# Modulation products moved between TensorE and VectorE in a two-layer attention, S5 and MLP kernel

## The chip, the cores and the metric

The kernel runs on one core of a Trainium2 chip. The metric is the device time of one execution in microseconds (us). TensorE does the matrix products, VectorE and ScalarE the element-wise work, SyncE issues nearly all loads, and 16 DMA engines move the data. In the profile PE is TensorE's matmul row, PEld its weight loads, DVE is VectorE, ACT ScalarE, POOL GpSimd, SP SyncE.

## What is computed

256 tokens of width 2048 go through two blocks. The first has two layers (differential attention, then forgetting attention), the second an S5 mixer with a GLU and a squared-ReLU MLP of width 8192. Each stage is modulated by vectors that come from products of one row with a wide matrix:

```python
mod = c_act @ w_mod[l] + b_mod[l]              # 2048 x 6144, for layer 0 and layer 1
shift, scale, gate = jnp.split(mod, 3, axis=-1)
h = x * (1.0 + scale[:, None]) + shift[:, None]
...
mod = c_act @ w_mod_kv + b_mod_kv              # keys' and values' stage, 2048 x 4096
...
sh1, sc1, gt1, sh2, sc2, gt2 = adaln(c, w_mod[layer], b_mod[layer])          # 2048 x 12288
csh1, csc1, cgt1, csh2, csc2, cgt2 = adaln(c_ctx, w_mod[layer], b_mod[layer])
```

The change is about where these products are made, and when.

## The kernel before, in words

**Weights.** All other matrices are streamed in tiles of 128 columns, called weights here: 64 for layer 0's input, 16 for its output, 16 for the keys and 16 for the values, 32 for layer 1's heads (two a head), 16 for its output, 32 for the GLU, 128 for the MLP. Each comes as two loads `w` of 512 KB; ScalarE makes a rounded copy `wh` (L134), VectorE the rest `wl` (L135), and TensorE multiplies (L163 to L165, `mm_t`; L200 to L202, `mm_n`; L176 and L177 in the MLP). Weights are prepared two ahead of their use.

**Modulation products.** Each product of 2048 outputs is cut in two halves of 1024 outputs, and each half in eight pieces. A piece is two loads `graw` of 128x1024 (L268, 512 KB each) and what is done with them (`gemv`):

- "pe": eight matmuls into `g` (L222), four at a time beside each other in column groups of 32. The profile has 16 records for one piece, since a float32 matmul has two.
- "dve": two operations `gacc <- graw, csilu, gacc` of 1024 columns on VectorE (L237); the first one of a half is on ScalarE (L235). A half that has any such piece closes with four matmuls of `gacc` (L246).
- The context's products (`mc`, with two result rows) are on TensorE whatever is asked for: `if eng == "pe" or nv == 2`.

There are 224 pieces in one queue, in the order m0 (32 pieces, layer 0's scale and shift), m02 (16), mk (32, keys), m1 (32), mc (32, context), m12 (16), m22 (16), m24 (32), m25 (16).

**When.** `weights()` calls `bg()` once for each weight. `bg` takes the next entry of the stage's policy (`P_L0A` for the first four heads of layer 0, `POL0` for its last four, `P_ON0` for its output, `P_KV` for keys and values, `P_QG` for layer 1's heads, `P_ON1` for its output, `P_GLU`, `P_MLP`): an engine's name issues the next piece, `None` issues none. The loads go out at once, the use of a piece one piece later. Some more pieces are issued at fixed places: 32 at the start, 6 before the keys (`BG_K`), 12 at the S5 scan (`BG_M`), `BG_V` after each of the first `BG_B` blocks of the S5 outputs. There are four buffers for `graw`.

**Context states.** When the last mc piece is used, `start_ctx` (asked at the start of each of layer 1's 16 heads) starts `ctx_states`: 41 steps, one for each later weight, with matmuls `inc` (L697) and VectorE operations on `ctx_ws` (L1337 to L1340); what is left is done after layer 1's output (`flush`).

**Between stages** VectorE makes the next stage's input tile by tile: `xres` (L1112, L1113) and `kL` (L420) before the keys; `U` (L1599), `xres` (L1600), `xn` (L1612) and `h` (L420) before the MLP.

The order in which one engine's instructions stand is set when the program is built, by a scheduler that lays all of them out; each engine then runs its own queue in order.

## Time and profile before

| | us |
|---|---|
| runs, unprofiled: median of three | 2543.52 (2540.8 to 2544.13) |
| the profiled execution: its own time | 2548.22 |
| its span in the trace | 2546.4 |
| TensorE busy | 2377.1 (93%) |
| VectorE busy | 1776.8 (70%) |
| ScalarE busy | 1239.5 (49%) |

The span is what the trace covers; 1.8 us of the profiled execution lie around it. Busy shares are means over stages with different limits, so each stage is read by its own window.

### The profile page before, as it was taken

The page shows a single profiled execution, that of the slowest core. Times are in us where ns is not written, and L with a number is a line of the kernel's source. Part 1 is how long each engine was busy: PE and PEld are TensorE (multiplying, and loading weights), DVE is VectorE, ACT ScalarE, POOL GpSimd, SP SyncE. Part 2 cuts the span into 40 slices and gives each one's busy share as a digit, 9 for nine tenths or more (in the row PEclk, how much of TensorE's full clock was granted, in tenths as well). Part 3 has the DMA queues.
Part 4 walks back from the last instruction along what each step waited for, and adds up shares of the span by engine and source line. Part 5 has one row for each costly group of instructions (what it writes and reads, how often), then busy time and mean ns, then how long its engine had stood idle before and what let it go on. Part 6 is the DMA issues. An engine that isn't in the chain of part 4 may idle for free.

```text
span 2546.4 us, 47968 instructions
## 1 busy us (share of the span) xinstructions
PE 2377.1 (93%) x18854; PEld 2051.9 (81%) x18854; DVE 1776.8 (70%) x3360; ACT 1239.5 (49%) x2153; POOL 118.8 (5%) x234
## 2 busy tenths in 40 slices
PE   5699999999899999999998874999899999999997
PEld 1299999999678888988886663898688888888885
DVE  3288778877775555778788997877854565665655
ACT  0554554444365556666653543544544443443442
POOL 0000000000002110000000021000000000000000
PEclk9999999999889999999998886999899999999998
DMA  9999999878769998878786762998366666666652
GB/s 325 339 344 325 323 321 344 306 275 316 265 226 342 327 332 290 296 248 290 257 273 230 233 210 77 334 320 279 118 186 187 186 187 191 189 190 184 189 182 91
DMA packets 203316, 644.66 MB, mean 253 GB/s; under 512 B 41009, under 2 KB 49457, under 8 KB 202705
## 3 DMA queue, kind: packets, MB, share of 16 engines
q1 hardware_dynamic: 195616, 620.47, 72.7%
q0 software_dynamic: 7472, 21.11, 2.1%
q8 instruction: 148, 2.42, 0.4%
q14 instruction: 80, 0.65, 0.1%
HBM read 613.71 MB, written 25.69 MB: 251 GB/s over the span
## 4 chain that ended last, share of the span: by engine, by line
PE 84%; DVE 9%; DMA 3%; ACT 2%; issue 1%; SPq 0%; POOL 0%; DVEq 0%; ACTq 0%; POOLq 0%
PE pj L176 18%; PE pj L163 12%; PE pj L164 12%; PE pj L165 12%; PE pj L177 9%; PE g L222 3%; PE pjv L200 3%; DMA graw<-in_w_mod 3%; PE pjv L201 2%; PE pjv L202 2%; DVE scan_t L1415 2%; DVE scan_t L1417 2%; DVE S L1419 2%; PE inc L697 2%; PE st L370 1%
## 5 line engine op out<-in xcount | busy, mean ns | idle before, releaser
L135 DVE TENSOR_TENSOR wl<-w,wh 128x1024 fp32r<-128x1024 f32 x631 | 770.0, 1224 | 465.2 <-ACT wh L134 457.2
L134 ACT CAST wh<-w 128x1024 fp32r<-128x1024 f32 x632 | 659.1, 1050 | 711.1 <-PE pj L176 283.0
L176 PE MATMUL pj<-h,wh 128*128 128x512 f32 x1024 | 362.9, 399 | 6.8 <-DVE h L420 5.0
L176 PE MATMUL pj<-d,wh 128*128 128x512 f32 x1024 | 360.3, 398 | 0.0
L237 DVE SCALAR_TENSOR_TENSOR gacc<-graw,csilu,gacc 128x1024 f32<-128x1024 f32 x211 | 270.2, 1281 | 27.4 <-DMA graw<-in_w_mod 18.6
L177 PE MATMUL pj<-h,wl 128*128 128x256 f32 x1024 | 287.5, 281 | 1.1 <-DVE wl L135 1.1
L177 PE MATMUL pj<-d,wl 128*128 128x256 f32 x1024 | 285.8, 280 | 0.0
L176 PEld LDWEIGHTS pj<-h,wh 128*128 128x128 f32 x1024 | 193.1, 189 | 55.8 <-issue 4.0
L176 PEld LDWEIGHTS pj<-d,wh 128*128 128x128 f32 x1024 | 192.0, 188 | 48.2 <-PE pj L177 1.7
L163 PE MATMUL pj<-hH,wh 128*128 128x256 f32 x768 | 221.6, 289 | 6.2 <-ACT hH L419 4.0
L165 PE MATMUL pj<-hH,wl 128*128 128x256 f32 x768 | 221.4, 289 | 0.5 <-DVE wl L135 0.5
L164 PE MATMUL pj<-hL,wh 128*128 128x256 f32 x768 | 221.1, 288 | 0.0
L222 PE MATMUL g<-graw,czc 128*32 128x256 f32 x1744 | 168.4, 469 | 49.6 <-DMA graw<-in_w_mod 48.0
L177 PEld LDWEIGHTS pj<-h,wl 128*128 128x128 f32 x1024 | 194.0, 189 | 1.5 <-DVE wl L135 1.5
L177 PEld LDWEIGHTS pj<-d,wl 128*128 128x128 f32 x1024 | 193.1, 189 | 0.4
L163 PEld LDWEIGHTS pj<-hH,wh 128*128 128x128 f32 x768 | 148.8, 194 | 9.8 <-ACT hH L419 4.1
L165 PEld LDWEIGHTS pj<-hH,wl 128*128 128x128 f32 x768 | 148.6, 194 | 4.5 <-issue 3.3
L164 PEld LDWEIGHTS pj<-hL,wh 128*128 128x128 f32 x768 | 148.9, 194 | 3.8 <-issue 3.7
L222 PEld LDWEIGHTS g<-graw,czc 128*32 128x32 f32 x1744 | 46.0, 119 | 129.4 <-DMA graw<-in_w_mod 105.5
L163 PE MATMUL pj<-h1H,wh 128*128 128x256 f32 x512 | 147.1, 290 | 0.3 <-ACT ctx_ws L1323 0.2
L164 PE MATMUL pj<-h1L,wh 128*128 128x256 f32 x512 | 146.4, 287 | 0.0
L165 PE MATMUL pj<-h1H,wl 128*128 128x256 f32 x512 | 146.0, 286 | 0.0
(480 smaller groups left out, 5201.4 us busy)
## 6 DMA issues: line engine op xcount, KB each, us to landing
graw<-in_w_mod SPq DMA_DIRECT2D x384, 512.0 KB, 5.8
w<-in_mlp_in SPq DMA_DIRECT2D x128, 512.0 KB, 4.3
w<-in_mlp_out SPq DMA_DIRECT2D x128, 512.0 KB, 4.3
w<-in_a_in SPq DMA_DIRECT2D x96, 512.0 KB, 6.3
graw<-in_w_kvmod SPq DMA_DIRECT2D x64, 512.0 KB, 6.6
w<-in_b_in SPq DMA_DIRECT2D x64, 512.0 KB, 5.8
w<-in_glu SPq DMA_DIRECT2D x56, 512.0 KB, 5.3
w<-in_a_v SPq DMA_DIRECT2D x32, 512.0 KB, 5.9
```

The lines of the kernel that those rows point to most:

```text
L134: nc.scalar.copy(h, src)
L135: (eng or (nc.gpsimd if next(self.spl) else nc.vector)).tensor_sub(l, src, h)
L163: self.nc.tensor.matmul(ps, h, aH, start=kt == order[0] and not opened, stop=False)
L164: self.nc.tensor.matmul(ps, h, aL, start=False, stop=False)
L165: self.nc.tensor.matmul(ps, l, aH, start=False, stop=kt == order[-1] and last)
L176: self.nc.tensor.matmul(ps, h, view(aH, 0, [[T, 2], [1, T]]), start=kt == order[0], stop=False)
L177: self.nc.tensor.matmul(ps[:, 0], l, aH, start=False, stop=kt == order[-1])
L200: self.nc.tensor.matmul(ps[:, i], aH[:, s], h, start=half == 0 and i == 0 and k == 0, stop=False)
L201: self.nc.tensor.matmul(ps[:, i], aH[:, s], l, start=False, stop=False)
L202: self.nc.tensor.matmul(ps[:, i], aL[:, s], h, start=False, stop=half == 1 and i == 1 and k == 7)
L222: nc.tensor.matmul(st["g"][32 * q:32 * q + 32], self.cz[c][:, ch * 2 + s], raw[s][:, q * 256:q * 256 + 256], start=st["n"] == 0, stop=ch = ...
L237: nc.vector.scalar_tensor_tensor(acc, raw[s], cc, acc, op0=MUL, op1=ADD)
```

## The change

Five policies and two numbers change, an entry of a policy may now be a tuple (several pieces at one weight), and layer 1's heads get a second policy, `P_QG2`, once the context's products are done.

```diff
-P_L0A = ('dve', 'pe')
-P_KV = ('dve', 'pe')
-P_QG = ('dve', 'dve', 'pe')
+P_L0A = ('dve', 'dve', 'dve', None)
+P_KV = ('dve',)
+P_QG = (('pe', 'pe'), 'pe')
+P_QG2 = ('dve', 'dve', None)
...
-P_ON1 = ('pe', 'dve', None)
-BG_V = 5
+P_ON1 = ('dve', None, None)
+BG_V = 2
...
-BG_B = 0
+BG_B = 3
...
             e = eng or next(self.pol)
-            if e and self.bgq and not (self.hold and self.bgq[0][0].startswith("m2")):
+            for e in e if isinstance(e, tuple) else (e,):
+                if not e or not self.bgq or self.hold and self.bgq[0][0].startswith("m2"):
+                    continue
                 name, gen, left = self.bgq[0]
...
                 self.steps = itertools.cycle(P_CTX)
+                self.policy(P_QG2, X_QG)
```

`P_L0A`, `P_KV`, `P_GLU` and the other policies are asked once for each weight, so the pieces can be counted:

| stage (weights) | before: pieces, of these on TensorE | changed: pieces, of these on TensorE |
|---|---|---|
| start | 32, 32 | 32, 32 |
| layer 0, heads 0 to 3 (32) | 32, 16 | 24, 0 |
| layer 0, heads 4 to 7 (32) | 24, 0 | 24, 0 |
| its output (16), then 6 | 18, 0 | 18, 0 |
| keys and values (32) | 32, 29 | 32, 18 |
| layer 1's heads (32) | 32, 14 | 30, 15 |
| its output (16) | 11, 6 | 6, 0 |
| S5 | 3 on VectorE and 12, 12 | 2 on VectorE and 18, 18 |
| GLU (32) | 28, 0 | 32, 0 |
| MLP (128) | 0, 0 | 6, 0 |

VectorE's queue between layer 0's output and the keys: `xres` and `kL` make the keys' input, `vprod` and `gen_ws` belong to a table of the S5 part, `lnb` is the layer norm's row. Before, at the eighth and ninth of the 16 tiles:

```order
L1113 TENSOR_TENSOR xres<-xres,lnb 128x256
L1112 TENSOR_TENSOR xres<-xres,lnb 128x256
L420 TENSOR_TENSOR kL<-u,kH 128x256
L635 TENSOR_TENSOR gen_ws<-vprod 128x32x16
L1113 TENSOR_TENSOR xres<-xres,lnb 128x256
L1112 TENSOR_TENSOR xres<-xres,lnb 128x256
L420 TENSOR_TENSOR kL<-u,kH 128x256
L554 TENSOR_TENSOR vprod<-gen_ws 128x512
```

In the changed program at the eighth tile (a line has a number there that is up to four higher):

```order
L557 TENSOR_TENSOR vprod<-gen_ws 128x512
L558 TENSOR_TENSOR vprod<-gen_ws 128x512
L238 SCALAR_TENSOR_TENSOR gacc<-graw,csilu,gacc 128x1024
L1116 TENSOR_TENSOR xres<-xres,lnb 128x256
L1115 TENSOR_TENSOR xres<-xres,lnb 128x256
L423 TENSOR_TENSOR kL<-u,kH 128x256
L638 TENSOR_TENSOR gen_ws<-vprod 128x32x16
L238 SCALAR_TENSOR_TENSOR gacc<-graw,csilu,gacc 128x1024
```

Between the norm's mean (`mr`) and the last `kL` there stood 8 operations `gacc`; now there are 16, one for nearly every tile.

VectorE's queue between the GLU and the MLP: `rr` is the end of a chain of small operations on 2 columns, and `U`, `xres`, `xn`, `h` make the MLP's input from it. Before:

```order
L1594 COPY rr<-ry 128x2
L1599 SCALAR_TENSOR_TENSOR U<-U,gs_18449,rrb 128x256
L1600 TENSOR_TENSOR xres<-xres,U 128x256
L1612 TENSOR_TENSOR xn<-xres,rrb 128x256
L1599 SCALAR_TENSOR_TENSOR U<-U,gs_18449,rrb 128x256
L1600 TENSOR_TENSOR xres<-xres,U 128x256
L1612 TENSOR_TENSOR xn<-xres,rrb 128x256
```

Changed:

```order
L1598 COPY rr<-ry 128x2
L238 SCALAR_TENSOR_TENSOR gacc<-graw,csilu,gacc 128x1024
L1603 SCALAR_TENSOR_TENSOR U<-U,gs_18214,rrb 128x256
L238 SCALAR_TENSOR_TENSOR gacc<-graw,csilu,gacc 128x1024
L1604 TENSOR_TENSOR xres<-xres,U 128x256
L238 SCALAR_TENSOR_TENSOR gacc<-graw,csilu,gacc 128x1024
L1616 TENSOR_TENSOR xn<-xres,rrb 128x256
L1603 SCALAR_TENSOR_TENSOR U<-U,gs_18214,rrb 128x256
L238 SCALAR_TENSOR_TENSOR gacc<-graw,csilu,gacc 128x1024
```

From the GLU's last `xy` to the fourth `U` no `gacc` stood there before; 15 stand there now: the pieces that are left over from the GLU, and the six that the MLP's policy issues.

SyncE's queue, the loads of the MLP's first weights (`w_0` and `w_1` are the two halves of one weight), changed program:

```order
L131 DMA w_1_20682<-in_mlp_in 128x1024
L269 DMA graw<-in_w_mod 128x1024
L131 DMA w_0_20729<-in_mlp_in 128x1024
L269 DMA graw<-in_w_mod 128x1024 x12
L131 DMA w_1_20735<-in_mlp_in 128x1024
```

Twelve loads `graw` now stand ahead of the second half of the MLP's fifth weight; before, the last `graw` stood ahead of the MLP's first weight.

## Rows read from the trace of the kernel before

**Rows 1.** Page: busy time by engine; the chain that ended last, by engine.
```profile
PE 2377.1 (93%) x18854; PEld 2051.9 (81%) x18854; DVE 1776.8 (70%) x3360; ACT 1239.5 (49%) x2153; POOL 118.8 (5%) x234
...
PE 84%; DVE 9%; DMA 3%; ACT 2%; issue 1%; SPq 0%; POOL 0%; DVEq 0%; ACTq 0%; POOLq 0%
```

**Rows 2.** Windows by stage: PE, PEld, DVE, ACT, POOL busy; clock, DMA share, GB/s.
```profile
301.70:362.20 60.50, 60.50 (x528) 55.97 (x528) 49.09 (x81) 31.02 (x56) 4.71 (x10) 1.00 0.94 333
...
698.00:720.00 22.00, 17.11 (x72) 15.03 (x73) 22.00 (x44) 10.55 (x23) 0.56 (x1) 0.58 0.69 212
...
749.00:780.00 31.00, 31.00 (x329) 27.46 (x322) 22.90 (x35) 21.80 (x43) 7.23 (x16) 1.00 0.98 348
...
841.00:964.00 123.00, 123.00 (x1293) 107.30 (x1289) 70.40 (x97) 64.53 (x123) 20.22 (x45) 1.00 0.96 332
964.00:1029.00 65.00, 65.00 (x553) 55.45 (x551) 34.81 (x59) 40.44 (x83) 6.46 (x12) 1.00 0.86 298
...
1490.00:1566.00 76.00, 45.02 (x416) 38.26 (x416) 76.00 (x373) 18.96 (x36) 18.00 (x24) 0.77 0.33 100
...
1777.00:1810.00 33.00, 20.68 (x90) 15.25 (x89) 26.00 (x76) 15.96 (x29) 0.00 (x0) 0.74 0.22 68
```

**Rows 3.** Windows of L222 alone, TensorE's modulation products: PE, PEld busy.
```profile
180.00:241.00 61.00, 5.11 (x64) 1.26 (x64) 1.00 0.92 319
...
749.30:841.10 91.80, 12.95 (x180) 5.05 (x176) 1.00 0.97 337
...
1241.80:1375.00 133.20, 7.12 (x96) 2.96 (x96) 1.00 0.78 262
```

**Rows 4.** Windows of VectorE alone, four weights of layer 0 each.
```profile
150.10:180.00 29.90, 27.13 (x42) 1.00 1.01 362
...
211.90:241.00 29.10, 25.71 (x42) 1.00 0.89 305
...
332.70:362.20 29.50, 25.70 (x44) 1.00 0.91 330
```

**Rows 5.** Timeline of VectorE before the keys: start us, us; idle before, releaser.
```profile
714.02 1.29 DVE L237 SCALAR_TENSOR_TENSOR gacc<-graw,csilu,gacc 128x1024 f32<-128x1024 f32 x1
715.22 0.43 DVE L1113 TENSOR_TENSOR xres<-xres,lnb 128x256 f32<-128x256 f32 x1
...
732.18 0.76 DVE L420 TENSOR_TENSOR kL<-u,kH 128x256 fp32r<-128x256 f32 x2 [0.17 <-ACT kH L419]
```

**Rows 6.** Timeline of TensorE there: the last wait on VectorE.
```profile
724.91 0.53 PE L165 MATMUL pj<-kH,wl 128*128 128x256 f32 x1 [1.19 <-DVE wl L135]
```

**Rows 7.** Timeline of VectorE at layer 1's end: the context's last operations, two norm steps.
```profile
1362.68 0.69 DVE L1337 TENSOR_TENSOR ctx_ws<-ctx_ws 128x512 f32<-128x512 f32 x1
1363.29 0.69 DVE L1338 TENSOR_TENSOR ctx_ws<-ctx_ws 128x512 f32<-128x512 f32 x1
...
1369.55 0.42 DVE L1337 TENSOR_TENSOR ctx_ws<-ctx_ws 128x256 f32<-128x256 f32 x1
1369.88 0.42 DVE L1338 TENSOR_TENSOR ctx_ws<-ctx_ws 128x256 f32<-128x256 f32 x1
...
1380.44 0.16 DVE L332 SCALAR_TENSOR_TENSOR rq<-rq,lv 128x2 f32<-128x2 f32 x1
1380.64 0.16 DVE L333 SCALAR_TENSOR_TENSOR rq<-rq 128x2 f32<-128x2 f32 x1
```

**Rows 8.** Chain that ended last, layer 1's heads: start us, us.
```profile
1044.64 1.90 PE inc L697 x32
```

**Rows 9.** Timeline of VectorE between GLU and MLP: start us, us; idle before, releaser.
```profile
1783.44 0.16 DVE L385 TENSOR_SCALAR var<-ysum 128x2 f32<-128x2 f32 x1 [2.95 <-PE ysum L380]
...
1789.32 0.48 DVE L1599 SCALAR_TENSOR_TENSOR U<-U,gs,rrb 128x256 f32<-128x256 f32 x1 [1.31 <-PE rrb L343]
...
1819.30 0.42 DVE L420 TENSOR_TENSOR h<-u,h 128x256 fp32r<-128x256 f32 x1 [0.77 <-ACT h L419]
```

**Rows 10.** All of `graw`: from issue to landing.
```profile
DMA to landing us min/median/max: 3.5/5.9/12.3
```

## The prediction

> **What bounds the kernel now.** I read the page first, then windows stage by stage, then the timelines of the places where stages meet. The page says TensorE: busy 93% of the span, and 84% of the chain that ended last, against 9% for VectorE [rows 1]. The windows split this. In the heads of layer 0, in the keys' and values' stage and in layer 1's heads TensorE is busy all the time (60.50 of 60.50 us, 31.00 of 31.00, 123.00 of 123.00, 65.00 of 65.00), at full clock [rows 2]. There a record taken from TensorE shortens the stage, as long as VectorE and the loads keep up; the reader should note that neither has much room: VectorE is at 81% in a head of layer 0, and the DMA share is 0.93 to 0.98. In three other stretches VectorE sets the pace: before the keys (698 to 720 us: VectorE 22.00 of 22.00, TensorE at a granted 0.58), in the scan (1490 to 1566: 76.00 of 76.00), and between GLU and MLP (1777 to 1810: 26.00 of 33.00, TensorE at 0.74) [rows 2]. What is put into VectorE's queue there is paid in full, unless it falls into a wait.
>
> **What the change moves.** By the count of the policies TensorE loses 16 pieces in layer 0, 11 in the keys' and values' stage and 6 in layer 1's output; it gains 1 in layer 1's heads and 6 in S5. The title's words don't hold in full: the start's 32 pieces stay on TensorE, and so do the 18 pieces of the context that come up among keys and values. VectorE gets what TensorE loses, and eight pieces of layer 0 pass down the line, until ten more come up in the GLU and the MLP.
>
> **Prices.** A piece on TensorE is 16 records: 5.11/64 x 16 = 1.28 us in layer 0, where it is split in two, 12.95/180 x 16 = 1.15 among keys and values, 7.12/96 x 16 = 1.19 in layer 1's output [rows 3]. An operation `gacc` takes VectorE 1.20 us from its start to the next one's (714.02 to 715.22), and a piece is two [rows 5].
>
> **The sum, term by term** (minus is faster).
>
> a) Layer 0, heads 0 to 3: 16 x 1.28 = -20.5. VectorE takes 24 pieces in place of 16, some 16 operations more. They come three pieces at a run and then none, so I look at four weights at a time. In the changed order 7, 8 and 7 operations stand in three such stretches that had 3 each; VectorE was busy 27.13 of 29.90, 25.71 of 29.10 and 25.70 of 29.50 us in them [rows 4]. With 4, 5 and 4 times 1.20 more it needs 31.9, 31.7 and 30.5 us, while TensorE, without two pieces, needs 27.3, 26.5 and 26.9: 13.4 us too much, if nothing is handed on to the neighbours, which have room. I take about half, 6: **-14.5**, bounds -20.5 and -7.1.
>
> b) Before the keys: 8 more operations in the row that makes `kL`, 9.6 us. TensorE waits for this row up to 724.91 [rows 6], the last `kL` starts at 732.18 [rows 5], so the last of them press less: **+8.4**, bounds 4.8 (the half that stands early) and 9.6.
>
> c) Keys and values: 11 x 1.15 = -12.7. The DMA share is 0.98 in the keys' part and 0.96 in the values' part [rows 2]; the same loads in less time leave hardly anything, and I give 2.7 back: **-10**, bounds -12.7 and -2.
>
> d) Layer 1's heads: one piece more, 1.2. Nine weights now carry 14 pieces. The stretch had a DMA share of 0.86 at 298 GB/s [rows 2], so the bytes fit, but four buffers must serve pairs, and a load takes 5.9 us to land [rows 10]. Half a landing in all, 3: **+4.2**, bounds 1.2 and 9.
>
> e) Layer 1's output: 6 x 1.19: **-7.1**, bounds -7.1 and -4. VectorE has no more pieces there than before.
>
> f) The context starts one head later, as its last piece is used at the tenth weight in place of the seventh. Two weights fewer are left for its steps, so its last block runs into the norm after layer 1's output: 4 or 5 operations of 0.61 us, 4 of 0.33, and as many each at about half of this and less [rows 7], some 6.5 us. Against it stand one `gacc` (1.20) that was there, and gaps of the norm's small operations, which start 0.20 apart and last 0.16 [rows 7], about 1.5 over some 28 of them. 16 matmuls `inc`, 1.90 us [rows 8], move from a stretch where TensorE is full to one where it waits. 6.5 - 1.2 - 1.5 - 1.9 = 1.9: **+1.9**, bounds 0 and 5.
>
> g) S5: the 6 added pieces stand in TensorE's queue behind the first blocks' outputs, while VectorE still scans; TensorE is busy 45.02 of 76.00 us there [rows 2]. **0**; without that cover 6 x 1.15 = 6.9.
>
> h) Between GLU and MLP: 15 operations `gacc` now stand in the one chain that the MLP waits for. Two waits can hide one or two, 2.95 us for `ysum` and 1.31 for `rrb` [rows 9]; 13 x 1.20 = 15.6 remain. Their loads come through four buffers, four in 5.9 + 1.2 us, which is 1.8 each and slower than 1.20 only where no other operation stands between. **+16**, bounds 12 (three more hidden) and 24 (every one waits for its load). TensorE can't take it back: the MLP's input is complete when the last `h` starts at 1819.30 [rows 9], and from there it is TensorE's own stage. The twelve loads ahead of the MLP's fifth weight cost nothing: four weights and a half are in before them, and TensorE needs several us for each.
>
> Sum: -14.5 + 8.4 - 10 + 4.2 - 7.1 + 1.9 + 0 + 16 = -1.1. Against the profiled execution's 2548.2 us that is 2547.1; that execution lay 4.7 above the median of the runs, 2543.5, so on their scale the changed kernel comes to **2542 us**: what TensorE is relieved of is handed back where VectorE sets the pace.
>
> **The rule that speaks otherwise.** The rows show VectorE full and TensorE at half its pace in exactly the places that get the most operations [rows 2]. The Trainium skill, Perfetto Trace Analysis, section "Identifying the Most-Contended Engine", says that a kernel is improved by improving the engine with the highest occupancy, which is TensorE here. By that alone the sum would be a, c, d and e without their deductions, -20.5 - 12.7 + 1.2 - 7.1 = -39, or 2504 us.
>
> **Rivals.** A measurement of this kernel tells a difference of about 0.2%, 5 us, from none.
>
> *No change, as summed:* 0.36.
>
> *The queues absorb it:* the deductions in a, c and d don't appear, since weights are prepared two ahead and VectorE can lag by that much. For it speaks that TensorE never waits in layer 0 with VectorE at 91% (27.13 of 29.90 [rows 4]). Sum: -20.5 + 8.4 - 12.7 + 1.2 - 7.1 + 1.9 + 16 = -12.8, 2531 us: 0.30.
>
> *VectorE becomes the bound of layer 0's first four heads* (the other side): VectorE's queue holds the splits `wl` and each head's softmax, which TensorE needs, behind `gacc`. If the overrun grows to eat the whole -20.5, a is 0 and the sum +13.4, 2557 us; from a = -8.4 on the kernel is more than 5 us slower. Against it: over a whole head the load is (49.09 + 4 x 1.20)/(60.50 - 5.11) = 97%, which is high but still under 1 [rows 2, 3]. 0.20.
>
> *Pairs of pieces wait for their loads* in layer 1's first nine weights: 14 pieces at 1 us of TensorE's time each, in place of the 3 in all, make it 2553 us. Against it: the DMA share of 0.86. 0.10.
>
> *Everything comes back that TensorE is relieved of* (that rule as a mechanism: b, f and h find waits to hide in): 2504 us. The waits that rows 9 show are 4.3 us, not 26. 0.04.
>
> **The range.** The two middle cases and the larger part of the next two lie within 2528 to 2557; what is left out is the last case and the outer parts of the second, third and fourth, under 2 in 10. For the likeliest case alone I would write 2538 to 2548. Faster by over 0.2%: 0.30 + 0.04 = 0.34; within it: 0.36; slower: 0.20 + 0.10 = 0.30.
>
> **What would show it.** a: heads 1 to 3 at some 56 to 58 us each in place of 60.5, with TensorE's first waits for `wl`. b: the weights of the keys start as before, and the fifth begins some 8 us later, measured from the first. c: the values' part little changed, the keys' part shorter by 4 to 10 us. f: `ctx_ws` between `mr` and the last `ry` of layer 1's norm. g: scan and S5 outputs as long as before. h: 33 us from the last GLU matmul to the full MLP grow to about 49; this is the step that I hold surest. The prediction is wrong if heads 0 to 3 lose less than 7 us, or if the stretch before the MLP grows by less than 10.

## The result, and the profile after

The changed kernel takes 2576.4 us (median; 2574.37 to 2578.54) against 2542.8 us: a ratio of 1.0133, 95% interval 1.0121 to 1.0146, so 33.6 us slower. The forecast was 2542 us, no change, with a range of 2528 to 2557. The profiled execution took 2575.43 us with a span of 2573.7, 27.3 us longer than the span before. The other 6.4 us lie between profile and median: the profiled execution of before was 5.4 us above its runs, this one 1.0 below.

TensorE was relieved, as the change says, and VectorE loaded. The page's first row, to compare with [rows 1]:

```profile
PE 2358.2 (92%) x18430; PEld 2045.4 (79%) x18430; DVE 1830.9 (71%) x3413; ACT 1240.4 (48%) x2152; POOL 124.4 (5%) x234
```

TensorE is busy 18.9 us less and the kernel is slower all the same. The Trainium skill, Perfetto Trace Analysis, section "Identifying the Most-Contended Engine", would have the engine with the highest occupancy optimized first. By the whole span that is TensorE, and here 18.9 us less of its busy time went with 27.3 us more of span. The Trainium skill, Perfetto Trace Analysis, section "Optimization Strategy", says that a kernel can have several regimes whose most contended engine changes, and with that the trace agrees, as the stages show.

Windows by stage, each from the first matmul of one stage to that of the next; layer 1's heads are also shown in two parts, which meet at their thirteenth weight. First the changed kernel (us; then PE, PEld, DVE, ACT, POOL busy; clock, DMA share, GB/s):

```profile
115.70:342.30 226.60, 220.45 (x1803) 215.40 (x1804) 199.82 (x282) 124.42 (x212) 17.89 (x32) 0.97 0.92 331
342.30:379.80 37.50, 31.96 (x256) 31.11 (x255) 33.95 (x61) 20.55 (x42) 5.33 (x8) 0.91 0.73 267
...
688.20:735.50 47.30, 37.23 (x197) 33.29 (x197) 44.29 (x78) 22.13 (x44) 1.99 (x5) 0.68 0.75 247
735.50:819.90 84.40, 84.30 (x831) 79.30 (x832) 71.27 (x94) 59.19 (x112) 16.76 (x31) 1.00 0.84 296
819.90:948.80 128.90, 124.53 (x1266) 105.83 (x1264) 68.90 (x92) 64.07 (x119) 20.12 (x41) 0.99 0.92 330
948.80:1249.80 301.00, 288.37 (x2480) 251.29 (x2480) 209.97 (x375) 181.88 (x376) 10.74 (x28) 0.96 0.77 258
948.80:1076.30 127.50, 122.27 (x1102) 98.46 (x1102) 63.41 (x112) 71.43 (x153) 9.49 (x26) 0.94 0.84 290
1076.30:1249.80 173.50, 166.11 (x1381) 152.83 (x1379) 146.57 (x264) 110.45 (x224) 1.25 (x2) 0.98 0.72 234
1249.80:1384.00 134.20, 130.32 (x1112) 113.21 (x1111) 100.99 (x176) 71.65 (x134) 3.70 (x6) 0.99 0.73 243
1384.00:1605.90 221.90, 149.63 (x1905) 114.68 (x1905) 195.08 (x883) 98.41 (x190) 31.26 (x40) 0.78 0.54 181
...
1766.00:1854.00 88.00, 61.99 (x367) 50.69 (x365) 77.83 (x138) 38.79 (x66) 0.53 (x2) 0.79 0.64 224
```

The same stages of the kernel before, where [rows 2] show only a part of them:

```profile
112.20:362.20 250.00, 245.06 (x2085) 225.55 (x2086) 197.75 (x307) 128.54 (x231) 17.93 (x38) 0.99 0.94 335
362.20:390.60 28.40, 28.40 (x250) 27.14 (x250) 16.78 (x21) 14.08 (x23) 1.43 (x4) 1.00 0.93 331
...
698.10:749.30 51.20, 44.46 (x309) 38.38 (x309) 40.70 (x79) 28.89 (x59) 2.00 (x5) 0.77 0.59 182
749.30:841.10 91.80, 91.80 (x966) 80.69 (x962) 58.80 (x84) 55.92 (x108) 18.50 (x40) 1.00 0.97 337
841.10:964.00 122.90, 122.90 (x1293) 107.30 (x1289) 70.40 (x97) 64.44 (x123) 20.12 (x45) 1.00 0.96 331
964.00:1241.80 277.80, 277.10 (x2403) 244.77 (x2401) 205.41 (x360) 183.13 (x377) 8.80 (x18) 0.99 0.83 280
964.00:1066.10 102.10, 101.93 (x905) 88.10 (x903) 61.52 (x98) 70.70 (x148) 6.46 (x12) 1.00 0.84 290
1066.10:1241.80 175.70, 175.17 (x1500) 156.67 (x1499) 143.89 (x263) 112.43 (x229) 2.34 (x6) 0.99 0.82 274
1241.80:1378.10 136.30, 134.24 (x1192) 115.12 (x1190) 106.19 (x198) 67.66 (x123) 2.44 (x6) 1.00 0.78 265
1378.10:1592.20 214.10, 143.35 (x1805) 113.44 (x1805) 192.29 (x861) 98.21 (x188) 31.38 (x38) 0.76 0.53 171
...
1752.70:1823.20 70.50, 56.34 (x354) 47.77 (x352) 54.76 (x118) 36.99 (x63) 0.00 (x0) 0.88 0.41 132
```

| stage | before | changed | difference | predicted |
|---|---|---|---|---|
| layer 0, first 36 weights (a) | 278.4 | 264.1 | -14.3 | -14.5 |
| keys and values (b + c) | 265.9 | 260.6 | -5.3 | -1.6 |
| layer 1's heads (d) | 277.8 | 301.0 | +23.2 | +4.2 |
| its output, up to the norm's mean `mr` (e) | 136.3 | 134.2 | -2.1 | -7.1 |
| norm and S5 (f + g) | 214.1 | 221.9 | +7.8 | +1.9 |
| last four GLU weights, first four of the MLP (h) | 70.5 | 88.0 | +17.5 | +16 |

The other stages add +0.5 together: the start +3.5, the rest of layer 0 +0.9, the GLU -0.4, the MLP -3.5. Of the 28 us by which the sum missed, 19 lie in layer 1's heads. TensorE's waits in values and heads, changed kernel (what it waited for: us in total, times, longest):

```profile
PE pj L164 <- ACT h1H L422: 4.4, 1, 4.4
PE pj L164 <- ACT ctx_ws L1327: 4.2, 1, 4.2
PE pv L1240 <- ACT ws L1236: 3.8, 2, 3.2
PE inc L700 <- DVE ws L1272: 1.4, 1, 1.4
PE g L223 <- DMA graw<-in_w_mod: 1.1, 1, 1.1
```

Before, the same stretch had 0.4 and 0.2 us. The first of these waits stands at the heads' first matmul, at 944.4 us; the other long ones come at 1065.4 (`pv`) and 1130.6 us (`ctx_ws`). Only 1.1 us are for a load of the pairs. Windows of TensorE in each of the three long waits and behind it (us, busy, clock, DMA share, GB/s):

```profile
944.40:948.80 4.40, 0.03 (x4) 0.84 1.00 393
948.80:955.00 6.20, 5.49 (x37) 0.56 0.56 199
1065.40:1068.60 3.20, 0.00 (x1) 0.73 1.00 391
1068.60:1077.00 8.40, 8.38 (x47) 0.50 0.72 269
...
1130.60:1134.80 4.20, 0.03 (x1) 0.63 0.96 254
1134.80:1142.00 7.20, 7.20 (x46) 0.74 0.73 237
```

The reader should see that these waits are paid nearly twice. Behind the three, 4.4 + 3.2 + 4.2 = 11.8 us, TensorE runs at a granted 0.50 to 0.74, and 6.2 x 0.44 + 8.4 x 0.50 + 7.2 x 0.26 = 8.8 us are lost. In the heads alone TensorE waited 301.0 - 288.4 = 12.6 us (the first of the three lies ahead of them, its clock in them). Before, it waited 0.7 us there and lost some 1.6 to the clock (39.1 us at a granted 0.96, from 1066.1 on). So of the 23.2 us 11.9 are waiting and some 7 are clock. The rest is work: counted by use and not by issue, TensorE makes 17 pieces in the heads where it made 14 (272 and 224 records), since of the 18 issued among keys and values only 16 are used there. These three are 3 x 1.19 = 3.6 us, and 11.9 + 7.2 + 3.6 = 22.7.

The two parts of the heads show more. TensorE's modulation products alone (PE, PEld busy) in the second part, in the changed kernel:

```profile
1076.30:1249.80 173.50, 0.00 (x0) 0.00 (x0) 0.98 0.72 234
```

and before:

```profile
1066.10:1241.80 175.70, 7.04 (x96) 2.62 (x96) 0.99 0.82 274
```

All 17 pieces now stand in the first part, where 8 stood before, and none in the second, where 6 stood. The first part grew from 102.1 to 127.5 us; of these 25.4 us nine pieces are 10.7, waits 5.2, and the clock behind the first two long waits 6.9 by the sum above. The second should have lost the six pieces' 7 us and lost 2.2, since TensorE waits there for 173.5 - 166.1 = 7.4 us, 0.5 before. Yet VectorE was given hardly more to do there: 25 operations `gacc`, 24 before, and 146.57 us busy, 143.89 before; in the heads as a whole it has 28, 32 before. What went away is TensorE's own work, which had lain over VectorE's delays; e11 and e12 below bear on this.

How the wait at 1130.6 comes about is read on ScalarE and VectorE (timelines; start us, us):

```profile
1129.64 0.40 ACT L1225 ACTIVATE ws<-ws,mx 128x128 f32<-128x128 f32 x1 [1.51 <-DVE mx L1224]
...
1130.04 1.77 ACT L1319 ACTIVATE ub<-uctx,ctx_ws 64x64 f32<-64x64 f32 x4
...
1134.14 1.07 ACT L1327 COPY ctx_ws<-inc 128x512 f32<-128x512 f32 x2
```

```profile
1129.00 0.41 DVE L1272 SCALAR_TENSOR_TENSOR ws<-tg,pj 128x256 f32<-128x256 f32 x1
```

TensorE's next matmul waits for `ctx_ws<-inc`, the eviction of the context's step, at 1134.14. On ScalarE that stands behind the softmax `ws<-ws,mx` and eight `ub` of the context; the softmax had waited 1.51 us for VectorE's maximum `mx`. On VectorE `ws<-tg,pj`, whose `tg` ScalarE wrote from 1125.59 to 1125.98, starts at 1129.00, behind a `gacc` (1125.80), operations of the context and of the softmax; TensorE's `inc` waited 1.37 us for it. So three queues in order have a part in this wait, each with something put in front; ScalarE's eight `ub` alone last 3.5 us.

### The profile page after: what moved, and what is told of

It reads as the page before. It is cut to its first block, busy times and chain, and to the rows that moved or that the text cites. A ratio compares the mean times of both kernels' runs of the same rounds, so it can differ in the third digit from the quotient of the medians.

```text
span 2573.7 us, 47239 instructions
## 1 busy us (share of the span) xinstructions
PE 2358.2 (92%) x18430; PEld 2045.4 (79%) x18430; DVE 1830.9 (71%) x3413; ACT 1240.4 (48%) x2152; POOL 124.4 (5%) x234
## 5 line engine op out<-in xcount | busy, mean ns | idle before, releaser
L238 DVE SCALAR_TENSOR_TENSOR gacc<-graw,csilu,gacc 128x1024 f32<-128x1024 f32 x264 | 337.5, 1279 | 27.6 <-ACT gacc L236 14.8
L223 PE MATMUL g<-graw,czc 128*32 128x256 f32 x1328 | 135.4, 497 | 53.9 <-DMA graw<-in_w_mod 51.9
L223 PEld LDWEIGHTS g<-graw,czc 128*32 128x32 f32 x1328 | 32.8, 123 | 123.6 <-DMA graw<-in_w_mod 109.4
```

The source lines that it names most:

```text
L223: nc.tensor.matmul(st["g"][32 * q:32 * q + 32], self.cz[c][:, ch * 2 + s], raw[s][:, q * 256:q * 256 + 256], start=st["n"] == 0, stop=ch = ...
L238: nc.vector.scalar_tensor_tensor(acc, raw[s], cc, acc, op0=MUL, op1=ADD)
```

## The experiments

Theory (V): in layer 1 VectorE has no room beside its part of the heads and of the context's steps, so a piece given to it comes back as a wait of TensorE, and the wait takes the clock with it; work handed on to a later stage ends in the same place or in the norm. Rivals: the pairs' loads hold up the weights' loads (P); ScalarE's queue makes the waits (A); each stage pays or gains just TensorE's time of its pieces (N, the sum of the prediction).

Stages in the profiles (us, by the first matmul of a weight), and the change of the median against the kernel before beside it. The start, the rest of layer 0, the GLU up to its last four weights and the rest of the MLP are left out. The profile of the kernel before lies 5.4 us above its runs, those of the others between 6.6 below and 3.1 above theirs, so the stages of a run do not add up to the change of its median. Times are rounded from finer ones, and a tenth can differ from the table above.

| run | layer 0, 36 weights | keys, values | layer 1's heads | output, norm, S5 | GLU's last, MLP's first 4 | median |
|---|---|---|---|---|---|---|
| before | 278.4 | 265.9 | 277.8 | 350.3 | 70.6 | |
| changed | 264.0 | 260.6 | 301.0 | 356.1 | 88.0 | +33.6 |
| e1_no_pairs | 262.5 | 261.6 | 277.8 | 385.6 | 87.9 | +38.1 |
| e2_later_on_pe | 263.6 | 262.2 | 309.8 | 352.4 | 91.6 | +37.4 |
| e3_tail_to_s5 | 263.2 | 261.0 | 300.7 | 353.6 | 68.8 | +18.7 |
| e4_l0_only | 263.9 | 260.6 | 275.4 | 373.8 | 71.7 | +14.3 |
| e5_l0_back | 278.0 | 266.1 | 296.6 | 348.3 | 70.1 | +17.8 |
| e6_kv_back | 263.4 | 260.5 | 293.3 | 355.2 | 88.3 | +22.8 |
| e7_l0_no_handing_on | 269.3 | 266.6 | 272.5 | 349.7 | 70.9 | -12.6 |
| e8_pairs_alone | 278.9 | 266.0 | 275.7 | 355.7 | 70.6 | +7.0 |
| e9_l0_and_half_earlier | 269.0 | 263.7 | 303.2 | 341.8 | 72.8 | +28.4 |
| e10_l0_all_vector | 269.4 | 264.4 | 277.8 | 350.6 | 69.5 | -10.0 |
| e11_repaired | 268.6 | 266.7 | 289.0 | 348.1 | 70.2 | -0.8 |
| e12_pe_between | 268.9 | 267.2 | 277.4 | 363.6 | 71.1 | +4.3 |
| e13_thin_gacc | 264.3 | 261.6 | 287.5 | 358.4 | 90.3 | +23.0 |
| e14_few_ub | 264.7 | 261.5 | 296.5 | 355.7 | 87.9 | +29.7 |
| e15_both_thin | 264.0 | 260.9 | 285.4 | 354.4 | 87.5 | +15.5 |

**e1_no_pairs**, the changed kernel with

```diff
-P_QG = (('pe', 'pe'), 'pe')
+P_QG = ('pe',)
```

> The changed kernel, but layer 1's heads take one piece a weight on TensorE until the context's products are done, in place of two and one in turn. In the changed kernel layer 1's heads took 301.0 us from their first weight to that of the output (277.8 before), and the last four weights of the values 37.4 us (30.8 before); TensorE stood idle there 4.39 us (first weight of the heads), 3.21 (twelfth) and 1.37 and 4.21 (eighteenth and nineteenth). Theory P (the pairs: their loads stand ahead of the weights' loads and take the four buffers): the first two waits go, the last four weights of the values come back to about 31 us, the kernel gains 12 to 18 us, about 2562. Rival V (VectorE: operations gacc among the context's steps make it late, whatever came before): the waits at the eighteenth and nineteenth weight stay in some form, the values' last weights come back too, and the whole gains less than 6 us, about 2572.

Measured 2580.3 us (ratio 1.0148, 1.0134 to 1.0161). Both missed. The wait of 4.39 us at the heads' first weight stayed, so it is not the pairs'. The heads did come back to 277.8 us, but the context's steps now start six weights later (the first `inc` at 1107.0 us, 1072.7 in the changed kernel) and more of them are done in output and norm instead; with S5 these take 29.5 us more. The work went where it had to be done sooner or later.

**e2_later_on_pe**, the changed kernel with

```diff
-P_QG2 = ('dve', 'dve', None)
+P_QG2 = ('pe', 'pe', None)
```

> The changed kernel with the pairs kept, but the pieces after the context's products go to TensorE (two weights of three) in place of VectorE: 15 pieces more for TensorE in layer 1's heads, 18 us by 1.19 us a piece, and 28 operations gacc fewer on VectorE. Theory V: the waits of TensorE after the twelfth weight (1.37, 4.21, 0.88, 0.57 us and the half clock behind them, some 11 us in all) vanish, so the heads grow by only some 7 us, to about 308 us, the kernel to about 2583. Theory P: these waits are not VectorE's doing, so the heads grow by the full 18 us, to 319, the kernel to about 2594.

Measured 2579.6 us (1.0144, 1.0128 to 1.0159); the heads 309.8 us, where V said 308 and P 319. TensorE's waits in the heads:

```profile
PE pj L164 <- ACT h1H L422: 4.4, 1, 4.4
PE g L223 <- DMA graw<-in_w_mod: 4.0, 3, 2.1
```

Beside these, only waits of 2.5 and 1.0 us are left. The waits for `ctx_ws` and for VectorE's `ws` are gone with the `gacc`: 15 pieces more on TensorE, 18 us by their own price, made the heads 8.8 us longer. V by the number, but the pieces also give TensorE work that covers any delay, whoever makes it; e13 to e15 take that apart.

**e3_tail_to_s5**, the changed kernel with

```diff
-BG_V = 2
+BG_V = 5
```

> The changed kernel with five pieces in place of two after each of the first three S5 blocks: 9 pieces more under the scan on TensorE, and of the 15 operations gacc between GLU and MLP only few remain. Theory T (the operations in the chain to the MLP cost what they last there): the stretch from the last four GLU weights to the fifth MLP weight, 88.0 us in the changed kernel and 70.6 before, comes back to 71 to 75 us, S5 costs nothing, and the kernel gains 13 to 17 us, about 2561. Rival S (TensorE has no room in S5, since it is late for the output of the last blocks): the scan and S5 outputs grow by up to 9 x 1.15 = 10 us and the kernel gains only 3 to 7 us, about 2571.

Measured 2560.9 us (1.0073, 1.0060 to 1.0085), 14.9 us less than the changed kernel, each against its own runs of before, as theory T had it. TensorE's waits between GLU and MLP, first in the changed kernel, then here:

```profile
PE pj L177 <- DVE h L423: 9.6, 4, 6.4
```

```profile
PE pj L177 <- DVE h L423: 4.9, 3, 3.7
```

TensorE's wait for `rr` fell from 5.5 to 1.1 us. The nine pieces in S5 are not quite free: from the norm to the last GLU weights the kernel takes some 5 us more (GLU up to its last four weights 169.3 us, 160.1 in the changed kernel; norm and S5 3.9 us less).

**e4_l0_only**, the kernel before with

```diff
-P_L0A = ('dve', 'pe')
+P_L0A = ('dve', 'dve', 'dve', None)
...
-BG_B = 0
+BG_B = 2
```

> The kernel before with layer 0's first four heads alone changed (three of four weights with a piece on VectorE), and the 8 pieces that this passes on taken up in S5 on TensorE (five after each of the first two blocks). Everything between keeps its policy, but the queue runs 8 pieces later there. If term a holds (measured 14.3 us over the first five heads in the changed kernel) and the scan hides the 8 pieces: 14 us faster than the kernel before, about 2529. Rival: the context's products, 8 pieces later in the queue, start the context's steps later in layer 1's heads, and these run into the norm behind its output; then 4 to 10 us of it come back, 2533 to 2539.

Measured 2556.5 us (1.0054, 1.0041 to 1.0066): slower, which neither had. Layer 0 gained its 14.5 us. But the eight pieces handed on start the context's steps later, and output, norm and S5 take 23.5 us more, the GLU up to its last four weights 6.2. TensorE's longest wait in that norm, 2.2 us before:

```profile
PE lnb L343 <- DVE rc L1105: 9.7, 1, 9.7
```

**e5_l0_back**, the changed kernel with

```diff
-P_L0A = ('dve', 'dve', 'dve', None)
+P_L0A = ('dve', 'pe')
```

> The changed kernel with layer 0's first four heads as before (a piece at every weight, VectorE and TensorE in turn), so all later pieces come 8 earlier in the queue: nearly nothing is left for the stretch before the MLP, and the context's steps start some weights earlier. Theory H (the 8 pieces handed on cost more than layer 0 saves): layer 0's first 36 weights grow by 14 us, the stretch before the MLP loses 14 to 17, layer 1's heads have 6 pieces fewer on TensorE (7 us), the norm behind layer 1's output loses 4: about 2562, with some 14 us to 20 us left over the kernel before. Rival W (VectorE's lag in layer 1's heads grows with the 36 operations gacc there, 28 in the changed kernel): the heads gain nothing and the kernel stays at 2568 or more.

Measured 2561.1 us (1.0071, 1.0058 to 1.0083): H in the total. Layer 0's whole gain can be given up, and the kernel is some 16 us faster than the changed one. In the heads W holds in part: they lose 4.4 us for six TensorE pieces fewer, 7.1 us by their price, and waits of 6.8 and 4.5 us stand there.

**e6_kv_back**, the changed kernel with

```diff
-P_KV = ('dve',)
+P_KV = ('dve', 'pe')
```

> The changed kernel with keys and values as before (VectorE and TensorE in turn): 7 pieces go back to TensorE, 8 us by 1.15 us a piece; no count of a later stage changes. Theory O (the wait of 4.39 us at the first weight of layer 1's heads and the half clock behind it come from the order that this policy gives ScalarE's queue): the last four weights of the values fall from 37.4 to 30 or 31 us and the kernel stays within 3 us of the changed one, 2574 to 2579. Rival: the wait belongs to what comes behind (the pairs' loads), stays, and the kernel takes 2583 to 2585.

Measured 2566.1 us (1.0087, 1.0074 to 1.0100). O was right on the wait: the values' last four weights take 29.8 us, and the 4.39 us are gone. The gain is larger than O said. Keys and values last 260.5 us with seven more pieces on TensorE and 260.6 without, so that move bought nothing in sum: the changed kernel's keys are 6.8 us shorter than those of e6 and its values 6.9 longer, 4.4 of it the wait. Taking the move back also shortens the heads by 7.7 us, but not at their start. Their first eleven weights take 106.8 us in e6 and 104.4 in the changed kernel; the next two take 18.1 in place of 32.5, as the wait of 3.2 us and the half clock behind it are gone there, and some 4 come back later, where waits of 3.4 and 4.5 us stand. ScalarE at the heads' start, changed kernel and e6:

```profile
944.50 0.37 ACT L250 COPY gs<-g 128x256 f32<-128x256 f32 x1
944.77 2.56 ACT L420 ACTIVATE u<-xres,m,s 128x256 f32<-128x256 f32 x5
...
948.38 1.01 ACT L422 CAST h1H<-u 128x256 fp32r<-128x256 f32 x3
```

```profile
935.23 2.58 ACT L420 ACTIVATE u<-xres,m,s 128x256 f32<-128x256 f32 x5
...
945.74 0.71 ACT L422 CAST h1H<-u 128x256 fp32r<-128x256 f32 x2
```

In the changed kernel the heads' first input `u` stands behind the eviction `gs` of the last piece, so TensorE, done at 944.4, waits for `h1H` until 948.8; in e6 `h1H` is written from 945.7 on, and TensorE reaches it at 946.3 without a wait. That the policy of the keys decides this place is, as far as these rows show, an effect of the scheduler's order and not of the price of a piece.

**e7_l0_no_handing_on**, the kernel before with

```diff
-P_L0A = ('dve', 'pe')
+P_L0A = ('dve', 'dve', 'dve', 'pe')
```

> The kernel before with 8 of layer 0's 16 TensorE pieces moved to VectorE in the first four heads (three weights on VectorE, the fourth on TensorE), so that no piece is handed on and no later stage changes. If what layer 0 gains is TensorE's time of these pieces, 8 x 1.28 = 10.2 us, with VectorE just keeping up since the heads are longer by the 8 pieces left: about 2532. Rival: VectorE falls behind as in the changed kernel (the norm of the fifth head waited 5.54 us there, and the clock fell behind it, 9.1 us in all), and the gain is 1 to 3 us, about 2540.

Measured 2530.7 us, ratio 0.9953 (0.9941 to 0.9965): the fastest of all, and as the count had it. Layer 0's first four heads:

```profile
113.20:354.60 241.40, 233.42 (x1961) 222.62 (x1962) 212.39 (x320) 130.68 (x235) 19.58 (x40) 0.98 0.96 350
```

The same 24 pieces are on VectorE as in the changed kernel, but TensorE's eight give it the time: no wait at the fifth head. By the profiles 9.1 us of the gain lie in layer 0 and 5.4 in layer 1's heads, whose counts are those of before; why these are shorter is not shown. e4 differs from e7 in these eight pieces alone (and in taking up ten later): not doing them in layer 0 saves 5.4 us there and costs 26.9 us in the whole, by the medians.

**e8_pairs_alone**: the kernel before with the two policies of layer 1's heads changed, and four pieces in S5 after each of the first two blocks.

```diff
-P_QG = ('dve', 'dve', 'pe')
+P_QG = (('pe', 'pe'), 'pe')
+P_QG2 = ('dve', 'dve', None)
...
-BG_V = 5
+BG_V = 4
...
-BG_B = 0
+BG_B = 2
```

> The kernel before with only the policies of layer 1's heads changed (pairs on TensorE until the context's products are done, then two of three weights on VectorE), and 8 pieces that are left over put into S5 on TensorE. TensorE has 5 pieces fewer in the heads (6 us), the context's steps start some three weights earlier, so the norm behind the output loses up to 3 us, S5 pays some 5 us for its 8 pieces. By the count alone 4 us faster, about 2538. Rival V (VectorE gets 33 operations gacc in place of 29, nearly all while the context's steps run, and TensorE waits for it as in the changed kernel): the heads lose nothing or grow, and the kernel takes 2545 to 2555.

Measured 2550.3 us (1.0028, 1.0018 to 1.0039), as V said: five pieces fewer on TensorE are worth 6 us and the heads lose 2.2; the output takes 5.3 us more (141.6 up to `mr`, 136.3 before). S5 did not pay for its eight pieces (214.1 us from `mr` to the GLU in both). The two spans are equal, though (2546.0 and 2546.4 us), so the stages do not show where the 7.0 us of the medians lie.

**e9_l0_and_half_earlier**, e7 and

```diff
-POL0 = ('dve', 'dve', 'dve', None)
+POL0 = ('dve', 'dve', 'dve', 'pe')
```

> The kernel before with three weights on VectorE and the fourth on TensorE in all eight heads of layer 0: the last four heads issue 8 pieces more (on TensorE, 8 x 1.28 = 10.2 us there), so everything behind comes 8 pieces earlier in the queue, the context's steps start some weights earlier and the GLU has 7 or 8 pieces fewer. Theory Q (a piece is dearer the later it stands: eight pieces handed on past layer 0 cost some 36 us by the two runs that differ in just this): handing eight forward gives back more than its 10 us, and the kernel is at 2520 to 2528. Rival: the dear thing was only the context's steps running into the norm, which the kernel before has nearly none of (2.2 us of waiting), so the 10 us are paid for little: 2533 to 2541.

Measured 2573.4 us (1.0121, 1.0105 to 1.0137): both far off. Output, norm and S5 do gain (341.8 us), but the context's steps now fall on the heads' first weights, where the S5 table is still being made:

```profile
PE kps L649 <- ACT gen_ws L646: 6.9, 3, 5.7
PE inc L697 <- ACT ub L1315: 5.3, 1, 5.3
```

and layer 0's last heads and output pay 15.4 us more than before for eight pieces. Earlier is not better by itself either.

**e10_l0_all_vector**, the kernel before with

```diff
-P_L0A = ('dve', 'pe')
+P_L0A = ('dve',)
```

> The kernel before with all 32 pieces of layer 0's first four heads on VectorE, none handed on. With three of four there VectorE was busy 212.4 of 241.4 us in these heads; 16 operations more by 1.20 make 231.6, while TensorE without 8 more pieces needs 231. Theory L (VectorE is then the limit, since its queue also holds what TensorE waits for): layer 0's first 36 weights lose less than 4 us against 269.3 with three of four, or grow, and the kernel is at 2527 to 2536. Rival: the queues absorb it, another 10 us, about 2521.

Measured 2535.0 us (0.9968, 0.9955 to 0.9980): theory L. Its 36 weights last 269.4 us and those of e7 269.3; TensorE's relief is lost for the most part in two waits for VectorE's `ry`, 8.9 us in all, the longer one 7.3.

**e11_repaired**, the changed kernel with

```diff
-P_L0A = ('dve', 'dve', 'dve', None)
+P_L0A = ('dve', 'dve', 'dve', 'pe')
-P_KV = ('dve',)
+P_KV = ('dve', 'pe')
```

> The changed kernel with keys and values as before and with the fourth weight of layer 0's first heads on TensorE, so that no piece is handed on past layer 0; the pairs, the thinner policy of layer 1's output and the six pieces more in S5 stay. From the run with only keys and values as before (2566): layer 0 takes 5 us more than there, the stretch before the MLP loses 14 to 17, the norm behind layer 1's output 4, TensorE has fewer pieces in the heads: about 2546. If the waits on VectorE in layer 1's heads grow with the 37 operations gacc there (28 before this), 2552 or more. Either way above the kernel before with layer 0's part alone (2531): what is left of the change in layer 1 and S5 costs 15 us or more.

Measured 2544.2 us (0.9998, 0.9989 to 1.0007), no change against before. e7 was 12.6 us under its runs of before and this is 0.8 under: 11.8 us are what the rest of the change costs (15 or more were expected).

**e12_pe_between**, e11 and

```diff
-P_QG2 = ('dve', 'dve', None)
+P_QG2 = ('dve', 'dve', 'pe')
```

> The run e11 with one entry changed: behind the context's products the third weight of three takes a piece on TensorE in place of none. TensorE has 8 pieces more in layer 1's heads (8 x 1.19 = 9.5 us), VectorE as many operations a weight as before (two weights of three). In e11 the heads took 289.0 us, and TensorE waited there 1.80, 1.06, 7.41 and 4.51 us. Theory V (VectorE's queue sets these heads: a weight from which TensorE's own piece is taken only ends earlier if VectorE can follow): the waits shrink by more than half, the heads stay within 3 us of 289, and with 8 pieces fewer left for the GLU the kernel stays at 2541 to 2547. Rival N (TensorE pays for each of its pieces, as the sum of the prediction reckons): the heads take 297 to 300 us, the kernel 2552 to 2555.

Measured 2548.5 us (1.0016, 1.0006 to 1.0026). The heads with these eight TensorE pieces more are 11.6 us shorter, not 9.5 longer as N had it, and not within 3 us as V had it. Windows of the heads in e11 and in e12:

```profile
954.80:1243.80 289.00, 273.13 (x2313) 245.12 (x2310) 218.02 (x376) 180.56 (x372) 7.74 (x16) 0.96 0.78 261
```

```profile
954.60:1232.00 277.40, 274.27 (x2453) 242.37 (x2450) 209.29 (x365) 182.14 (x376) 11.01 (x18) 1.00 0.85 291
```

TensorE waits 15.9 us in e11 and 3.1 in e12, and the clock is back at 1.00: beside the context's steps eight pieces on TensorE cost the heads nothing, and the waits are gone. Five `gacc` fewer on VectorE in the heads (33, 38 in e11) may have a part in it. But a wait of 9.58 us for an eviction of the context's step stands in the output instead (148.4 us up to `mr`, 133.3 in e11), so the total is 4 us above e11 and misses V's range by 1.5 us.

**e13_thin_gacc**, the changed kernel, with a switch that is on from the start of the context's steps to the last head:

```diff
-                        nc.vector.scalar_tensor_tensor(acc, raw[s], cc, acc, op0=MUL, op1=ADD)
+                        n = 64 if self.thin else 1024
+                        nc.vector.scalar_tensor_tensor(acc[:, 0:n], raw[s][:, 0:n], cc, acc[:, 0:n], op0=MUL, op1=ADD)
```

> The changed kernel; in layer 1's heads, from the start of the context's steps to the last head, VectorE's operations gacc take 64 of their 1024 columns, so that part of the modulation products is left out there; loads, TensorE and ScalarE keep their work. VectorE is relieved of about 28 x 1.1 = 31 us. Theory V (the gacc between the other operations make VectorE late): the waits of TensorE for ctx_ws, ws and inc behind the twelfth weight (4.2, 1.4, 0.9, 0.6 us and some 2 us of clock) go, the heads fall from 301.0 to 292 us or less, the kernel to about 2567. Rival A (ScalarE's queue, with the 16 operations ub of each context block in front, makes them): the heads stay within 3 us of 301.

Measured 2564.7 us (1.0081, 1.0060 to 1.0102); the heads 287.5 us, 13.5 less than in the changed kernel. From 1000 us to their end TensorE waits once, at the twelfth weight, and in the second part of the heads it is busy all the time, at full clock:

```profile
PE pv L1243 <- ACT ws L1239: 3.8, 1, 3.8
```

```profile
1075.30:1235.90 160.60, 160.60 (x1368) 148.93 (x1366) 120.38 (x259) 108.77 (x223) 1.54 (x2) 1.00 0.74 251
```

12.9 of the 13.5 us come there (173.5 in the changed kernel). The waits for `ctx_ws` and `inc` and the later ones for `ws` are gone, with TensorE's and ScalarE's work as it was: they need the `gacc`, as V says. The kernel before has as many `gacc` there (24), so this shows what they cost where TensorE has no pieces to fill the waits, not that the change brought more of them.

**e14_few_ub**, the changed kernel with

```diff
-            for i in range(8):
+            for i in range(1):
                 for s in range(2):
                     r = slice(64 * s, 64 * s + 64)
                     nc.scalar.activation(self.ub[r, i, s], u[r, i], AF.Identity, scale=sf[r, i, 0, b:b + 1],
```

> The changed kernel with 2 of the 16 operations ub of each of the context's eight blocks on ScalarE, so that the context's states are computed from a part of their input; the rest as it was. ScalarE is relieved of 14 x 0.44 = 6.2 us a block. Rival A: the waits at the twelfth weight (3.2 us, behind five ub) and for the eviction ctx_ws (4.2, behind eight ub) go, with the half clock behind them (4.2 and 1.9): the heads fall from 301.0 to 287 to 291 us. Theory V: only the first of these goes, 293 to 296 us.

Measured 2571.3 us (1.0106, 1.0085 to 1.0128); the heads 296.5 us, 4.5 less: V's number nearly, not A's. The wait at the twelfth weight shrinks from 3.21 to 1.96 us, so ScalarE's `ub` are a part of that one. The wait for `ctx_ws` falls too, from 4.2 to 1.4 us, as A had it, while others for `ws`, 2.0 and 1.9 us, are left. So the wait for `ctx_ws` needs both, the `gacc` and the `ub`.

**e15_both_thin**: both edits.

> Both cuts together: thin gacc in the heads and 2 of 16 ub. If these two fill what the heads lost behind their first weights, all waits go but the one at the first weight (0.7 us of it and 2.7 of clock in the heads) and the load's 1.1 us: 301.0 - 10.8 - 6.1 = 284 us or less. If it stays above 290, the lengthening is neither's, but of the chain of the softmax itself, which TensorE's shorter weights no longer cover.

Measured 2557.1 us (1.0058, 1.0037 to 1.0078); the heads 285.4 us, 15.6 less than in the changed kernel. Behind their first weights one wait of 1.98 us is left. Of the 23.2 us that is two thirds, most of it VectorE's. The 7.6 us that are left over the kernel before hold the three pieces more (3.6) and 4.2 us of waits in all (0.7 before), with the clock behind them.

## Why the prediction was wrong

**The step that failed** is term d, layer 1's heads: +4.2 with bounds 1.2 and 9, measured +23.2. It set the pieces off against each other, 15 for 14, at TensorE's own time, and added half a landing for the pairs' loads. Three things in this were wrong. By use there are three pieces more, 3.6 us. The nine that stand earlier are paid for, 10.7 us, but the six that were taken from the context's steps gave back 2.2 us and not 7, since TensorE waits 7.4 us there, 0.5 before, for VectorE and what hangs on it. And the half clock behind the waits, some 7 us more than before, stood nowhere in the sum. The condition that I set at the start, a record taken from TensorE shortens the stage "as long as VectorE and the loads keep up", was looked at from 964 to 1029 us alone [rows 2], where VectorE is busy 34.81 of 65.00 us. That window ends where the context's steps begin; in the heads' second part VectorE is busy 143.89 of 175.70 us already in the kernel before, in a queue through which each head's softmax goes twice.

What the waits hang on is shown in part. Without the length of the `gacc` among the context's steps 13.5 us go (e13), with ScalarE's `ub` thinned as well 15.6 (e15); eight TensorE pieces put among the steps take 11.6 away in the heads, if not in the whole (e11 to e12). The wait at the heads' first matmul goes with ScalarE's order (e6). That e6 also ends the wait at the twelfth weight is not explained by a count, and its 7.7 us were not taken together with the 15.6, so that they add up is not shown.

**a** was right in the sum and not in the way, so that the match is luck. TensorE gained 23.4 us over the first 32 weights, more than the bound of 20.5, and lost 9.1 over the next four. The wait is one, at the fifth head's norm, and the clock behind it:

```profile
PE rb L346 <- DVE ry L337: 5.5, 1, 5.5
```

**What is handed on** was priced at TensorE's own time and h. e4 against e7 shows 26.9 us for eight pieces. By the profiles, whose spans differ by 24.3 us, 11.1 lie between `mr` and `mr<-ry`, where the context's steps run into the norm, 5.0 in layer 1's output, 8.0 in the rest of norm and S5 and 6.2 in the GLU. In S5 e4 also has ten pieces more on TensorE, so the last two are not the context's alone.

**b and c** came to -5.3 in place of -1.6, and b's mechanism was wrong. The row of `kL` did get longer, from 36.2 to 46.6 us (first `xres` at 686.11, last `kL` at 732.66; before, 696.03 and 732.18), as reckoned. But TensorE then had 16 us of own work left before and has 2 now (749.3 and 735.5 for the fifth weight): its own matmuls covered the row, and I had named only the waits. c held in the keys, whose later weights take 84.4 us in place of 91.8, and was lost in the values, 128.9 in place of 122.9: 4.4 of these 6.0 us are the wait at the heads' first matmul. Together that is -1.4 in place of -10. By use TensorE has thirteen pieces fewer there (29 and 16), not eleven.

**e** gave 2.1 of its 7.1 us: a wait of 2.88 us at one of its matmuls (1296.7 us), the clock behind it, and 32 records of `inc` more, some 2 us (14.92 in place of 12.88). **f** had the right place and too small a size: from `mr` to `mr<-ry` it takes 7.1 us in place of 2.9, and TensorE's wait for `lnb` 6.42 in place of 2.24. **g** was right: e5 and e11 have the same 18 pieces in S5, no late context step, and take 213.8 and 214.7 us from `mr` to the GLU, 214.1 before; so I put the 7.8 us of the changed kernel down to f, predicted at 1.9. **h** was right in place and size: 15 `gacc`, +17.5 us; e3 took it back.

Of the rivals, VectorE as the bound came nearest, but in layer 1; in layer 0 it cost one wait. The pairs' loads made TensorE wait 1.1 us. That all comes back was furthest off.

Left open: how much of the 6.4 us between profiles and medians belongs to a stage, and what the scheduler's order does by itself, with the same counts; every edit here, those of e13 to e15 too, also lays the queues out anew.

## What to carry to other kernels

A piece of work is not worth its own time but what the stretch makes of it. Where VectorE was busy 82% and the chain to TensorE ran through its queue, six pieces taken from TensorE gave back 2.2 of 7 us, and eight put there made the stage 11.6 us shorter, though the next one longer. So read the other engine's load in the very stretch that gains or loses work, to its end, and not in the stage's first window; and count work where it is used, not where it is issued. Work that is put off is paid at the price of the place where it ends up: the version that won moved only as much as layer 0 could take and handed nothing on. Reckon a wait of several us with the clock behind it.

## What the runs showed of the hardware

The granted clock fell to 0.50 in the 8.4 us behind a wait of 3.2 us, that is TensorE at 1.2 GHz, and to 0.56 in 6.2 us behind 4.4. The Trainium skill, TensorE: Matmul & The Clock Gate, part 1, says that the throttled state is the default and activity releases it; the trace agrees, and shows here that behind the three long waits this cost three quarters of the waiting again (8.8 us behind 11.8). It is not the same behind every wait: behind 5.5 us at 354.6 the clock was 0.82 for 9.9 us, which is 1.8 lost, and behind the 1.1 us for a load of the pairs it stayed at 1.00.

Four MLP weights take 22.60 us in one stretch and 22.20 in another, at the same granted clock, here in the kernel before:

```profile
1936.40:1959.00 22.60, 22.60 (x130) 19.61 (x129) 11.14 (x12) 9.49 (x12) 0.00 (x0) 1.00 0.61 186
2116.60:2138.80 22.20, 22.20 (x130) 19.42 (x129) 13.17 (x16) 8.44 (x8) 0.00 (x0) 1.00 0.63 190
```

VectorE does not go with it: its operations `wl` last 1.22 to 1.23 us in both stretches. The MLP, the same instructions in all profiles, lasts from 717.4 to 723.2 us by how much of it falls into either; what sets it is open. A comparison by one profile each carries some 5 us of this.
